# Gate units at three per four key tiles, their high products on VectorE, later transposes, early operand loads and a fourth raw value tile

## The chip, the core and the metric

The program runs on one core of a Trainium2 chip. TensorE (PE in the profile; PEld is its weight loads) multiplies, VectorE (DVE), ScalarE (ACT) and GpSimd (POOL) work on tiles of 128 partitions, and transfers are issued from SyncE's queue (SP) or from GpSimd's. The metric is the device time of one execution in microseconds, the median of several runs.

## The reference, cut

Two layers of attention and feed-forward are followed by two layers of a short convolution or a windowed attention, each with a product-key expert layer ("peer"). Only the two expert layers bear on this change:

```python
q  = (t @ w_q).reshape(n_tok, 8, 2, 128)                   # 256 tokens, 8 heads, 2 halves
sc = einsum("thpd,hpnd->thpn", q, subkeys)                 # 128 keys in each half
sv, si = top_k(sc, 16)
cand = sv[:, :, 0, :, None] + sv[:, :, 1, None, :]         # 16 x 16 pairs of keys
top_v, pos = top_k(cand, 16)
idx = si0[pos] * 128 + si1[pos];  g = softmax(top_v)       # 8 x 16 experts for a token
h = einsum("cd,ced->ce", xc, u_tab[idx])
out = einsum("ce,ced->cd", g * gelu(h), v_tab[idx])
```

## The kernel before

All weights come as 512 KB tiles of 128 partitions by 1024 float32 through one `Stream`. A tile is loaded by SP into a raw tile (L145), ScalarE casts it to a high part `whi` (L156) and VectorE, or GpSimd for tiles marked so in `specs`, subtracts to the low part `wlo` (L165). I call the two together the split. TensorE then takes three products: low weight by high activation, high by low, high by high. In the expert layers there are three raw tiles and three pairs of split tiles (`CAP[0]`), and each is used again in turn; `next` emits the splits up to two tiles ahead of the tile that TensorE is given.

An expert layer (`peer`) is computed densely for 224 of the 256 tokens (`TD`), with gates that are zero where an expert is not chosen; the other 32 tokens (`TG`) fetch their experts' rows by indirect transfers. Its stages follow each other on TensorE:

- **Queries.** Eight pairs of `w_pq` tiles give the queries; `scores` compares them with the keys.
- **Keys.** 128 `peer_u` tiles, the key tiles, give all experts' inner products by `feat_block` (24 matmuls a tile, L505, L506, L510). `keep_h` applies Gelu for each pair of tiles: for tokens without gates yet into `st` (L1549), for the first `td` tokens that have gates into `tmp` (L1552), which VectorE multiplies onto `st` (L1553).
- **Values.** 128 `peer_v` tiles are multiplied by the gated activations (`experts_out`, L1633 and L1636, 16 matmuls a tile).

What is not matrix work of the key stage is written as generators in a list `bg`: `rank_keys` for each head, `rank_pairs` for each block of 128 tokens, then `gates`, then `gather`. After each weight tile `spend` runs them until a budget is used (1.2 after a first tile of a pair, 1.4 after a second); each yield names a cost by which the budget falls. That is the order on every engine, since the program is scheduled by hand.

`rank_pairs` ends with three transposes on TensorE (L1446, L1448) and three copies by VectorE into `ii`, `gg` and `gl` (L1463 to L1465). `gates` works in 56 units of four tokens. For each, VectorE writes two one-hot matrices (L1488), GpSimd multiplies the column one by the gate's high part `gg` (L1490), and the same matrix is multiplied by the low part `gl` on GpSimd for even units (L1492) or by four ScalarE instructions for odd ones (L1497). Two units later TensorE sums them in eight matmuls (L1505, L1506), and the result goes to `st`: by ScalarE where no key tile has been yet (L1513), by VectorE onto what is there (L1515). A unit costs 9.0, so one unit stands after each key tile. The sums lie in PSUM banks named `acc`, the inner products of the keys in banks named `sd`, four of each.

`gather` first loads 32 rows of `x` in four copies and a norm gain into `work` (L290), multiplies them on VectorE (L1583), and then goes through 32 rows of `peer_ur` and 32 of `peer_v`, one 512 KB indirect transfer each (L1574) and one VectorE instruction each (L1589, L1598), over a ring of three tiles. What is left of it is run by `next(rows)` in `experts_out`, one step for each pair of value tiles and a second one where `jj % 16 == 8`.

## Time and profile before

| what | value |
|---|---|
| median of 3 runs | 2541.38 us (2536.73 to 2543.12) |
| the profiled execution | 2538.01 us |
| its span, first to last instruction | 2536.2 us |
| PE, DVE, ACT, POOL busy | 93%, 77%, 51%, 30% of the span |
| moved by DMA | 496.75 MB, 196 GB/s on the mean |

The profiled execution is 1.8 us longer than its span and 3.4 us under the median. The first expert layer lies from 743 to 1575 us of the span and the second from 1697 to 2536 us: two thirds of the whole. The shares of busy time are means over all stages, and VectorE's 77% hides a stage in which it is busy for 95%; so the profile is read by stretches, with TensorE's matmuls counted in each.

### The profile page before, as it was taken

What the parts mean: (1) busy time and instruction counts of PE and PEld (TensorE: products, weight loads), DVE (VectorE), ACT (ScalarE), POOL (GpSimd) and SP (SyncE); (2) the same over time, 40 slices, a digit from 0 to 9 for tenths busy, and PEclk for the clock granted to TensorE, in tenths of its full rate; (3) what the DMA queues carried; (4) which work ended last, traced back from release to release, by engine and by line L of the source; (5) the groups of instructions that cost most, each with busy time, mean ns of one, the idle gap of its engine ahead of it and who ended that gap; (6) DMA issues with size and microseconds to landing.
All of it is one profiled execution on the core that took longest, in us unless ns stands there. A gap on an engine that the chain in (4) does not pass through costs nothing.

```text
span 2536.2 us, 45120 instructions
## 1 busy us (share of the span) xinstructions
PE 2369.3 (93%) x17454; PEld 2224.7 (88%) x17454; DVE 1958.3 (77%) x3386; ACT 1294.3 (51%) x2170; POOL 748.8 (30%) x498
## 2 busy tenths in 40 slices
PE   8999989999999999888999999999999888999998
PEld 6789978899999998888988898889998888988897
DVE  5778776887868989995777776757989995777775
ACT  5555556555544455553444454645445553444454
POOL 0112123111011247663333310411247663333300
PEclk9999999999999999998999999999999998999999
DMA  7345642555545554447888876525654447888874
GB/s 240 100 147 198 209 147 83 173 195 190 180 149 173 183 168 141 143 134 246 297 298 292 289 244 191 170 93 164 189 170 140 143 141 241 301 289 293 302 246 147
DMA packets 141229, 496.75 MB, mean 196 GB/s; under 512 B 17185, under 2 KB 20897, under 8 KB 140754
## 3 DMA queue, kind: packets, MB, share of 16 engines
q1 hardware_dynamic: 121254, 426.11, 51.7%
q0 software_dynamic: 19232, 67.22, 7.3%
q8 instruction: 138, 2.26, 0.4%
q10 hardware_dynamic: 528, 0.52, 0.1%
q14 instruction: 77, 0.63, 0.1%
HBM read 491.07 MB, written 1.08 MB: 194 GB/s over the span
## 4 chain that ended last, share of the span: by engine, by line
PE 46%; DVE 24%; DMA 13%; issue 8%; ACT 7%; POOL 2%; SPq 0%; ACTq 0%; POOLq 0%; DVEq 0%
DMA raw<-peer_v 9%; DVE wlo L165 8%; PE sd L505 7%; PE sd L506 7%; PE sd L510 7%; ACT whi L156 4%; DMA raw<-peer_u 3%; PE acc L300 3%; PE acc L1633 3%; DVE oh L1488 3%; PE acc L301 3%; PE acc L302 3%; PE sd L1633 3%; DVE st L1553 3%; PE acc L1636 2%
## 5 line engine op out<-in xcount | busy, mean ns | idle before, releaser
L156 ACT CAST whi<-raw 128x1024 fp32r<-128x1024 f32 (+1 forms) x776 | 803.4, 1042 | 619.9 <-DMA raw<-peer_v 239.1
L165 DVE TENSOR_TENSOR wlo<-raw,whi 128x1024 fp32r<-128x1024 f32 (+2 forms) x687 | 881.4, 1296 | 301.6 <-ACT whi L156 285.3
L505 PE MATMUL sd<-hTh,wlo 128*128 128x224 f32 (+1 forms) x3176 | 765.8, 283 | 49.2 <-DVE wlo L165 25.5
L506 PE MATMUL sd<-hTl,whi 128*128 128x224 f32 (+1 forms) x3176 | 752.1, 279 | 0.6 <-DVE hTl L306 0.6
L505 PEld LDWEIGHTS sd<-hTh,wlo 128*128 128x128 f32 x3176 | 612.1, 193 | 59.2 <-DVE wlo L165 27.4
L506 PEld LDWEIGHTS sd<-hTl,whi 128*128 128x128 f32 x3176 | 612.1, 193 | 2.9 <-DVE hTl L306 1.0
L510 PE MATMUL sd<-hTh,whi 128*128 128x224 f32 (+1 forms) x3176 | 430.4, 278 | 0.0
L510 PEld LDWEIGHTS sd<-hTh,whi 128*128 128x128 f32 x3176 | 396.5, 192 | 0.0
L165 POOL TENSOR_TENSOR wlo<-raw,whi 128x1024 fp32r<-128x1024 f32 (+1 forms) x89 | 220.5, 2482 | 399.3 <-ACT whi L156 396.0
L1633 PE MATMUL acc<-ahl,whi 128*128 128x448 f32 x1024 | 256.0, 371 | 32.7 <-ACT whi L156 28.0
L1633 PE MATMUL sd<-ahl,whi 128*128 128x448 f32 x1024 | 252.0, 366 | 0.0
L1633 PEld LDWEIGHTS acc<-ahl,whi 128*128 128x128 f32 x1024 | 174.8, 190 | 47.5 <-ACT whi L156 34.0
L1633 PEld LDWEIGHTS sd<-ahl,whi 128*128 128x128 f32 x1024 | 193.0, 188 | 14.5
L1497 ACT ACTIVATE oh<-oh,gl 128x128 f16<-128x128 f16 x224 | 74.1, 431 | 183.7 <-POOL oh L1490 183.7
L1574 POOL DMA_INDIRECT work<-peer_v,idx x64 | 101.0, 1579 | 221.8 <-DVE work L1598 178.1
L1636 PEld LDWEIGHTS acc<-ahl,wlo 128*128 128x128 f32 x1024 | 153.3, 191 | 14.5 <-DVE wlo L165 5.5
L1488 DVE TENSOR_TENSOR oh<-ii,iota 128x512 f16<-128x512 f16 x224 | 161.3, 759 | 0.0
L1636 PE MATMUL acc<-ahl,wlo 128*128 128x224 f32 x1024 | 157.9, 275 | 2.6 <-DVE wlo L165 2.5
L1636 PE MATMUL sd<-ahl,wlo 128*128 128x224 f32 x1024 | 159.0, 276 | 0.0
L1490 POOL TENSOR_TENSOR oh<-oh,gg 128x512 f16<-128x512 f16 x112 | 118.3, 1057 | 117.4 <-DVE oh L1488 98.2
L1574 POOL DMA_INDIRECT work<-peer_ur,idx x64 | 97.6, 1525 | 185.2 <-DVE work L1589 158.0
L1636 PEld LDWEIGHTS sd<-ahl,wlo 128*128 128x128 f32 x1024 | 137.2, 194 | 0.0
(317 smaller groups left out, 3324.5 us busy)
## 6 DMA issues: line engine op xcount, KB each, us to landing
raw<-peer_u SPq DMA_DIRECT2D x256, 512.0 KB
raw<-peer_v SPq DMA_DIRECT2D x256, 512.0 KB
raw<-w_up SPq DMA_DIRECT2D x88, 512.0 KB
raw<-w_down SPq DMA_DIRECT2D x36, 512.0 KB
raw<-w_pq SPq DMA_DIRECT2D x32, 512.0 KB
raw<-w_da SPq DMA_DIRECT2D x24, 512.0 KB
raw<-w_cin SPq DMA_DIRECT2D x24, 512.0 KB
raw<-w_da_o SPq DMA_DIRECT2D x8, 512.0 KB
```

The source lines that it names most:

```text
L156: self.nc.scalar.copy(hi[:, c], raw[:, c])
L165: e.tensor_tensor(lo[:, c], raw[:, c], hi[:, c].bitcast(F32), op=ALU.subtract)
L300: mm(out, sl, mh, start=start, stop=False)
L301: mm(out, sh, ml, start=False, stop=False)
L505: mm(out, lo[:, c], sh[:, kbase + k, ts], start=(k == 0), stop=False)
L506: mm(out, hi[:, c], sl[:, kbase + k, ts], start=False, stop=False)
L510: mm(out, hi[:, c], sh[:, kbase + k, ts], start=False, stop=(k == nk - 1))
L1488: nc.vector.tensor_tensor(o, two(ii[:, c, ts]), bc(self.iota[:, None], [P, 2, P, 2]), op=ALU.is_equal)
L1490: nc.gpsimd.tensor_tensor(high, cols, two(gg[:, ts]), op=ALU.mult)
L1574: nc.gpsimd.indirect_dma_start(out=ring[s % 3], out_offset=None, in_=tables[s // ns], in_offset=off)
L1633: mm(ot[f][:, 0:2 * TD], w[0][:, f * P:(f + 1) * P], a, start=start, stop=stop)
L1636: mm(ot[f][:, 0:TD], w[1][:, f * P:(f + 1) * P], a[:, 0:TD], start=False, stop=False)
```

## The change

Six edits, all in the two expert layers:

- `gates` yields 1.75 in place of 9.0, so that three units stand after four key tiles, and `spend` has 1.5 and 1.7 up to the pair `n` = 19.
- The high products go from GpSimd to VectorE. GpSimd keeps the low products of every fourth unit, and ScalarE takes those of three units in four. GpSimd splits no key tile from the 24th on (before: every fourth of all 128).
- The transposes with their copies become a function `turn`, which is called later: that of the first block between the two halves of the second block's pair ranking, that of the second block after the second gate unit.
- The rows of `x` and the norm gain are loaded at the pair `n` = 11, and not when the gather starts.
- `keep_h` writes Gelu in place, in PSUM, and VectorE multiplies from there; `tmp` goes away.
- `ii`, `gg` and `gl` become parts of one tile `aux`, which, once the gates are done, is a fourth raw tile for every fourth `peer_v` tile. The split tiles stay three.

In `experts_out` a pair's second gather step moves from ahead of the pair to between its two tiles.

```diff
         for j, (_, kind, _) in enumerate(specs):
             k = kind
...
+            x = False
+            if kind == 3:
+                k, fourth = 0, (fourth + 1) % 4
+                x = fourth == 0
+            r, rb = place("x", 1, j) if x else place(("raw", k), self.CAP[k], j)
+            n, nb = place(k, self.CAP[k], j)
+            self.where.append((k, n, x))
+            self.before.append(rb)
+            self.free.append(nb)
...
+        if x and part == 0:
+            return self.extra
...
-            ii = ph.tile([P, 2, TD], F16, name="ii")
-            gg = ph.tile([P, TD], F16, name="gg")
-            gl = ph.tile([P, TD], F32, name="gl")
+            aux = ph.tile([P, D], F32, name="aux")
+            ii = aux[:, 0:TD].bitcast(F16).rearrange("p (c t) -> p c t", c=2)
+            gg = aux[:, TD:TD + TD // 2].bitcast(F16)
+            gl = aux[:, 2 * TD:3 * TD]
...
                     top16([(tv[:, h], posv[:, h], cand[:, h]) for h in range(h0, h0 + 4)])
                     yield 2.4
+                    if turns:
+                        turns.pop()()
...
-                        nc.gpsimd.tensor_tensor(high, cols, two(gg[:, ts]), op=ALU.mult)
-                        if n % 2 == 0:
+                        nc.vector.tensor_tensor(high, cols, two(gg[:, ts]), op=ALU.mult)
+                        if n % 4 == 0:
                             nc.gpsimd.tensor_tensor(cols, cols, two(gl[:, ts]), op=ALU.mult)
-                    if n % 2 == 0 and 0 <= n - 1 < NG:
+                    if n % 4 != 1 and 0 <= n - 1 < NG:
...
-                    yield 9.0
+                    if n == 1:
+                        turns.pop()()
+                    yield 1.75
...
-                    tmp = ph.tile([P, 2, TD], F32, tag="tmp", bufs=1, name=self.nm("tmp"))
-                    nc.scalar.activation(tmp[:, :, 0:td], pv[:, :, 0:td], AF.Gelu)
-                    nc.vector.tensor_tensor(st[:, jj:jj + 2, 0:td], st[:, jj:jj + 2, 0:td], tmp[:, :, 0:td],
+                    nc.scalar.activation(pv[:, :, 0:td], pv[:, :, 0:td], AF.Gelu)
+                    nc.vector.tensor_tensor(st[:, jj:jj + 2, 0:td], st[:, jj:jj + 2, 0:td], pv[:, :, 0:td],
...
-                for q in quarter:
-                    self.load(xr[q], self.x[last, 1])
-                self.load(ring[2], self.ins["ffn_norm_g_2"][layer:layer + 1, :].to_broadcast([P, D]))
                 fetch(0)
                 fetch(1)
-                yield 0.0
...
             for n in range(8 + P // 2):
+                if n == 11:
+                    for q in quarter:
+                        self.load(work[q, 3], self.x[last, 1])
+                    self.load(work[:, 2], self.ins["ffn_norm_g_2"][layer:layer + 1, :].to_broadcast([P, D]))
...
-                        spend(1.2)
+                        spend(1.5 if n < 20 else 1.2)
...
-                        spend(1.4)
+                        spend(1.7 if n < 20 else 1.4)
...
+            self.ws.extra = aux
             self.experts_out(a_split, rows, work[:, 3], area, g_name, g_row, final)
...
-                pool[0] = j % 4 == 1
+                pool[0] = j < 24 and j % 4 == 1
...
-                s.append((i["peer_v"][layer][:, j, :], 0, False))
+                s.append((i["peer_v"][layer][:, j, :], 3, False))
```

The scheduling by hand decides where the units stand. On VectorE, in the middle of the first layer's gates, before (`oh` are the one-hot matrices and products, `wlo` a split tile's low part, `st` the gated activations):

```order
L1488 TENSOR_TENSOR oh_10372<-ii,iota 128x512 x2
L1515 SCALAR_TENSOR_TENSOR st<-acc_11868,st 128x76x4
L165 TENSOR_TENSOR wlo_11930<-raw_11785,whi_11929 128x1024
L1553 TENSOR_TENSOR st<-st,tmp_11960 128x2x120
L1488 TENSOR_TENSOR oh_10372<-ii,iota 128x512
L1488 TENSOR_TENSOR oh_10373<-ii,iota 128x512
L1515 SCALAR_TENSOR_TENSOR st<-acc_11917,st 128x78x4
L1488 TENSOR_TENSOR oh_10373<-ii,iota 128x512 x2
L1515 SCALAR_TENSOR_TENSOR st<-acc_11966,st 128x78x4
L165 TENSOR_TENSOR wlo_12028<-raw_11883,whi_12027 128x1024
```

and now:

```order
L1511 TENSOR_TENSOR oh_10090<-aux,iota 128x512 x2
L1513 TENSOR_TENSOR oh_10090<-oh_10090,aux 128x512
L1538 SCALAR_TENSOR_TENSOR st<-acc_12180,st 128x84x4
L181 TENSOR_TENSOR wlo_12245<-raw_12114,whi_12244 128x1024
L1511 TENSOR_TENSOR oh_10090<-aux,iota 128x512
L1511 TENSOR_TENSOR oh_10091<-aux,iota 128x512
L1513 TENSOR_TENSOR oh_10091<-oh_10091,aux 128x512
L1538 SCALAR_TENSOR_TENSOR st<-acc_12233,st 128x84x4
L181 TENSOR_TENSOR wlo_12290<-raw_12147,whi_12289 128x1024
L1577 TENSOR_TENSOR st<-st,sd_12191 128x2x140
L181 TENSOR_TENSOR wlo_12323<-raw_12196,whi_12322 128x1024
L1511 TENSOR_TENSOR oh_10091<-aux,iota 128x512 x2
```

Each unit has a third product on VectorE, every tile's low part is here, and one tile in four has no unit behind it. On the whole there are 79 low parts on VectorE between the first one-hot matrix and the gather's first product (L1583), where 44 were, and 37 products with Gelu in place of 28. TensorE has the 56 units over 75 key tiles in place of 56 and 15 key tiles behind them in place of 25. The gates begin nine tiles earlier.

On GpSimd, in the first layer's gates, before:

```order
L1490 TENSOR_TENSOR oh_10373<-oh_10373,gg 128x512
L165 TENSOR_TENSOR wlo_11586<-raw_11443,whi_11585 128x1024
L1490 TENSOR_TENSOR oh_10374<-oh_10373,gg 128x512
L1492 TENSOR_TENSOR oh_10373<-oh_10373,gl 128x512
L1490 TENSOR_TENSOR oh_10374<-oh_10374,gg 128x512
```

and now, all that it does from the last index copy to the end of the layer's gather:

```order
L1472 DMA idx<-st 32x32
L1473 DMA gt<-st 32x32
L1515 TENSOR_TENSOR oh_10090<-oh_10090,aux 128x512 x14
L1598 DMA work<-peer_ur,idx 128x1024 x32
L1598 DMA work<-peer_v,idx 128x1024 x32
```

GpSimd's 56 high products, half of its low ones and its splits are gone from the gates. On SP, around the loads of `x` and the gain, before:

```order
L145 DMA raw_13150<-peer_u 128x1024
L145 DMA raw_13183<-peer_u 128x1024
L290 DMA work<-x 32x1024 x4
L290 DMA work<-ffn_norm_g 128x1024
L145 DMA raw_13224<-peer_u 128x1024
```

and now, where they stand 100 rows earlier:

```order
L161 DMA raw_8855<-peer_u 128x1024
L161 DMA raw_8886<-peer_u 128x1024
L306 DMA work<-x 32x1024 x4
L306 DMA work<-ffn_norm_g 128x1024
L161 DMA raw_8932<-peer_u 128x1024
```

They have moved past some 100 key tiles, from the gather's start into the ranking of the keys.

## Rows read from the trace of the kernel before

**Rows 1.** By stretches, L505 alone: length, PE, PEld busy (count), clock, DMA share, GB/s
```profile
795.80:938.00 142.20, 91.48 (x384) 75.90 (x385) 0.96 0.58 179
938.00:1141.00 203.00, 105.78 (x441) 84.48 (x442) 1.00 0.47 141
1141.00:1170.20 29.20, 12.96 (x48) 10.50 (x48) 0.77 0.74 229
1170.20:1225.40 55.20, 35.13 (x152) 29.13 (x152) 1.00 0.79 269
1749.80:1888.00 138.20, 88.88 (x384) 73.81 (x384) 1.00 0.59 180
1888.00:2093.00 205.00, 105.58 (x441) 84.28 (x441) 1.00 0.46 142
2093.00:2122.50 29.50, 13.17 (x48) 10.67 (x48) 0.77 0.72 225
```

**Rows 2.** Unbroken stretches, all engines: length, PE, PEld, DVE, ACT, POOL, clock, DMA, GB/s
```profile
786.00:806.00 20.00, 20.00 (x178) 20.00 (x177) 15.85 (x75) 10.77 (x17) 2.39 (x1) 1.00 0.52 159
1500.00:1550.00 50.00, 50.00 (x321) 47.74 (x320) 31.78 (x32) 27.05 (x31) 0.00 (x0) 1.00 0.69 218
```

**Rows 3.** Timeline of PE: a gate unit's first matmul, and the next key tile's
```profile
1109.13 0.23 PE L1505 MATMUL acc<-oh 128*128 128x128 f16 x1
...
1109.62 0.35 PE L505 MATMUL sd<-hTh,wlo 128*128 128x224 f32 x1
```

**Rows 4.** Ranking and gates of the first layer, all engines, columns as in rows 2
```profile
763.00:938.00 175.00, 169.33 (x1457) 168.34 (x1456) 149.94 (x511) 86.02 (x113) 38.14 (x24) 0.97 0.56 175
938.00:1141.00 203.00, 182.69 (x1766) 177.53 (x1764) 193.72 (x227) 111.81 (x270) 141.36 (x95) 1.00 0.47 141
```

**Rows 5.** Waits from 770 to 938 us: us in total, times, longest
```profile
PE sd L1448 <- DVE st L1442: 4.8, 2, 3.0
```

**Rows 6.** Groups, 928 to 1147 us: busy us, mean ns | idle, releasers
```profile
L1488 DVE TENSOR_TENSOR oh<-ii,iota 128x512 f16<-128x512 f16 x112 | 79.8, 752 | 0.0
L165 DVE TENSOR_TENSOR wlo<-raw,whi 128x1024 fp32r<-128x1024 f32 x45 | 78.6, 1746 | 13.6 <-ACT whi L156 7.8 <-issue 5.4 <-ACT st L1549 0.4
L1553 DVE TENSOR_TENSOR st<-st,tmp 128x16 f32<-128x16 f32 (+27 forms) x28 | 32.8, 1172 | 0.0
...
L1490 POOL TENSOR_TENSOR oh<-oh,gg 128x512 f16<-128x512 f16 x56 | 58.7, 1048 | 59.6 <-DVE oh L1488 48.9 <-PE acc L1506 8.5 <-DVE st L1515 2.2
L1492 POOL TENSOR_TENSOR oh<-oh,gl 128x512 f16<-128x512 f16 x28 | 52.4, 1870 | 2.2
...
L1497 ACT ACTIVATE oh<-oh,gl 128x128 f16<-128x128 f16 x112 | 37.0, 430 | 89.6 <-POOL oh L1490 89.6
```

**Rows 7.** By line: shortest/median/longest ns; last row a group, 1147 to 1225 us
```profile
L1488 DVE TENSOR_TENSOR oh<-ii,iota x224: 407/412/2610, 928.8 to 2089.9; 128x512 f16<-128x512 f16 x112
L1515 DVE SCALAR_TENSOR_TENSOR st<-acc,st x112: 345/457/576, 942.4 to 2096.1; 128x192 f32<-128x192 f32 x4, 128x200 f32<-128x200 f32 x4, 128x208 f32<-128x208 f32 x4, 128x216 f32<-128x216 f32 x4
L1553 DVE TENSOR_TENSOR st<-st,tmp x80: 601/1115/2785, 947.5 to 2175.8; 128x448 f32<-128x448 f32 x26, 128x16 f32<-128x16 f32 x2, 128x32 f32<-128x32 f32 x2, 128x48 f32<-128x48 f32 x2
...
L165 DVE TENSOR_TENSOR wlo<-raw,whi 128x1024 fp32r<-128x1024 f32 x18 | 21.8, 1222 | 21.7 <-ACT whi L156 21.7
```

**Rows 8.** Waits at the gather's start, 1138 to 1176 us
```profile
DVE work L1583 <- DMA work<-ffn_norm_g: 12.0, 1, 12.0
```

**Rows 9.** Value stage, all engines: both layers with gather, and the fullest 25 us
```profile
1225.40:1475.00 249.60, 234.32 (x1444) 219.47 (x1445) 188.05 (x207) 113.74 (x134) 79.02 (x50) 0.99 0.84 294
2180.40:2430.00 249.60, 235.41 (x1455) 218.70 (x1455) 189.56 (x207) 113.58 (x135) 78.40 (x50) 1.00 0.84 296
2378.50:2403.50 25.00, 24.35 (x151) 22.55 (x150) 20.14 (x20) 10.73 (x13) 8.84 (x6) 1.00 0.92 329
```

**Rows 10.** Ranking, L165 alone: DVE and POOL busy (count)
```profile
763.00:938.00 175.00, 55.23 (x45) 30.99 (x13) 0.97 0.56 175
```

**Rows 11.** Issues of the loads of `x` on SP: shortest, median, longest ns
```profile
L290 SPq DMA_DIRECT2D work<-x x8: 527/603/1199, 1147.2 to 2101.6; - x8
```

More of the change, by code (lines that the diff above doesn't have):

```diff
@@ L117, in __init__, with place @@
         self.todo = []
-        self.where, self.before = [], []
-        seq = [[], [], []]
-        ring = 0
+        self.where, self.before, self.free = [], [], []
+        seq = {}
+        ring = fourth = 0
+        def place(key, cap, j):
+            q = seq.setdefault(key, [])
+            q.append(j)
+            return (len(q) - 1) % cap, q[-1 - cap] if len(q) > cap else -1
         for j, (_, kind, _) in enumerate(specs):
@@ L125, in __init__ @@
                 k = 1 if kind and ring >= self.CAP[0] else 0
-            self.where.append((k, len(seq[k]) % self.CAP[k]))
-            self.before.append(seq[k][-self.CAP[k]] if len(seq[k]) >= self.CAP[k] else -1)
-            seq[k].append(j)
+            x = False
[7 more added lines that the diff above has]
+            self.free.append(nb)
     def widen(self, pool):
@@ L168, in _open @@
     def _open(self, j):
-        k = self.where[j][0]
-        return (self.local if k == 2 else self.pools[k]) is not None
+        k, _, x = self.where[j]
+        return (self.extra if x else self.local if k == 2 else self.pools[k]) is not None
     def fill(self, n=None):
@@ L178, in _ready @@
         j = self.n_split
-        return j < self.n_dma and j < self.i + lead and self.before[j] < done
+        return j < self.n_dma and j < self.i + lead and self.free[j] < done
     def ahead(self, n, held):
@@ L1443, in rank_pairs @@
                 yield 0.6
-                pt = self.bank()
-                for c in range(2):
-                    nc.tensor.transpose(pt[:, c * P:(c + 1) * P], sel[:, c].rearrange("p h k -> p (h k)"),
-                                        self.ident)
-                nc.tensor.transpose(pt[:, 2 * P:3 * P], ge.rearrange("p h k -> p (h k)"), self.ident)
                 if tb == 1:
@@ L1459, in rank_pairs, with turn @@
                         nc.gpsimd.dma_start(gt[q], gef[last, q])
-                n = min(P, TD - tb * P)
-                ts = slice(tb * P, tb * P + n)
-                pi, pg = pt[:, 0:2 * P].rearrange("p (c t) -> p c t", c=2)[:, :, 0:n], pt[:, 2 * P:2 * P + n]
-                nc.vector.tensor_copy(ii[:, :, ts], pi)
-                nc.vector.tensor_copy(gg[:, ts], pg)
-                nc.vector.tensor_tensor(gl[:, ts], pg, gg[:, ts], op=ALU.subtract)
-                yield 0.8
+                def turn():
+                    pt = self.bank()
+                    for c in range(2):
+                        nc.tensor.transpose(pt[:, c * P:(c + 1) * P], sel[:, c].rearrange("p h k -> p (h k)"),
+                                            self.ident)
+                    nc.tensor.transpose(pt[:, 2 * P:3 * P], ge.rearrange("p h k -> p (h k)"), self.ident)
+                    n = min(P, TD - tb * P)
+                    ts = slice(tb * P, tb * P + n)
+                    pi, pg = pt[:, 0:2 * P].rearrange("p (c t) -> p c t", c=2)[:, :, 0:n], pt[:, 2 * P:2 * P + n]
+                    nc.vector.tensor_copy(ii[:, :, ts], pi)
+                    nc.vector.tensor_copy(gg[:, ts], pg)
+                    nc.vector.tensor_tensor(gl[:, ts], pg, gg[:, ts], op=ALU.subtract)
+                turns.append(turn)
+            turns = []
             state = {"j": 0, "t": 0, "b": 0.0}
@@ L1642, in experts_out @@
             nxt = a_split(jj + 2)
-            next(rows, None)
-            if jj % 16 == 8:
-                next(rows, None)
             for c in range(2):
+                if c == 0 or jj % 16 == 8:
+                    next(rows, None)
                 w = self.ws.next()
@@ L1681, in experts_out @@
         self.ws.ahead(2, 0)
+        self.ws.extra = None
         turn(1)
```

4 lines of the change are left out of this document (2 added, 2 removed).

## The prediction

> **What bounds the kernel now.** I looked first at the two expert layers by stretches, counting the L505 matmuls in each, because these are eight to a key tile and so turn a stretch into a number of tiles [rows 1]. Then I took a price for a tile from a stretch in which TensorE never stops [rows 2]: 178 matmuls in 20 us, 24 to a tile, so 2.70 us for a key tile; 321 in 50 us, 16 to a tile, so 2.49 us for a value tile. A gate unit adds 9.62 - 9.13 = 0.49 us on TensorE [rows 3]. The reader is to see how far each stretch lies above its price:
>
> - Ranking: 384/8 = 48 tiles, 48 x 2.70 = 129.6 us; measured 142.2 and 138.2. Lost: 12.6 and 8.6.
> - Gates: 55 tiles, each with a unit, 55 x 3.19 = 175.5; measured 203 and 205. Lost: 27.5 and 29.5.
> - Start of the gather: 6 tiles and the last unit, 16.7; measured 29.2 and 29.5. Lost: 12.5 and 12.8. The granted clock is 0.77 there.
> - The next 19 tiles: 51.3; measured 55.2. Lost: 3.9, which nothing in the change aims at.
> - Values with gather [rows 9]: 1444/16 = 90.3 tiles, 224.7 us, and 1455/16 = 90.9, 226.4; measured 249.6 each. Lost: 24.9 and 23.2.
>
> So some 81 us in each layer are time in which TensorE, the bound, waits, or runs at a lower clock after a wait. What it waits for differs by stretch. In the gates VectorE is busy for 193.7 of 203 us [rows 4], and its instructions are long: a low part takes 1746 ns on the mean where it takes 1222 after the gates, a one-hot matrix 752 where the shortest take 407, a product with Gelu 1172 where the shortest, of the full width, takes 601 [rows 6, 7]. GpSimd is busy for 141 us of the same stretch, and ScalarE stands for 89.6 us behind GpSimd's high products [rows 4, 6]. In the ranking TensorE waits twice for the last step before the transposes [rows 5]. At the gather's start VectorE waits 12.0 us for the gain, with the low parts of the next tiles queued behind it [rows 8].
>
> **The change part by part.**
>
> *Gates.* They take 75 tiles now: 75 x 2.70 + 56 x 0.49 = 229.9 us on TensorE. VectorE, at undisturbed durations [rows 7]: 75 low parts x 1.22 = 91.5; 56 units x three products x 0.41 = 68.9; 56 x 0.457 (L1515) = 25.6; 37 products with Gelu x 0.4 = 15 (they grow from almost nothing to 0.60; 22 if all were of the full width). Sum 201. The third product has no row on VectorE; it has L1488's size and types and the same kind of broadcast, so I take 0.41, with 0.75, L1488's mean in company, as the other end (+19). The product that reads PSUM has no row of its own either; L1515 reads PSUM too and is not slow, so I take the price of L1553 undisturbed. GpSimd keeps 14 products of 1.87 [rows 6]; each may hold VectorE for nothing or for its whole length, 0 to 26; I take 20, near the upper end, because VectorE's instructions are long exactly where GpSimd works. That makes 221 of TensorE's 230 us: tight, but under it. ScalarE gets 14 units more at 37.0/28 = 1.32 us, 18.5, and 20 more casts, 21, to 151 of 230, and its wait for GpSimd goes. Gelu into PSUM I price like Gelu into `tmp`; its bank stays taken until VectorE's product, which is covered by the other three banks, and an uncovered wait would be that product's 0.6 us a pair. Lost after: 5 us, between 0 and 23.
>
> *Ranking.* Nine tiles fewer stand beside the same ranking. VectorE's part without the low parts is 149.9 - 55.2 = 94.7 us [rows 4, 10], of which some 4 are the first gate units and 4 to 11 time lost to GpSimd's splits, half of which remain; I take 87. 40 low parts x 1.23 = 49. Together 136 us beside 49 tiles, whose TensorE time is 175 - 12.6 - 9 x 2.70 = 138. VectorE goes from 86% to nearly full, so I do not expect the loss to vanish: 8 us a layer, between 3 and 15. Deferring the transposes removes the 4.8 us of waits [rows 5] and the slow clock behind them; they still cost TensorE the same three matmuls, and VectorE's three copies wait for these with the next low part queued behind them, which one unit of lead covers.
>
> *Loads of `x` and the gain.* VectorE's wait of 12.0 us goes. What is late next is the first gathered row, which GpSimd can issue before VectorE reaches it. Lost at the start after: 1.5 us, between 0 and 5. The five transfers, 1 MB, now stand in SP's queue in front of key tiles in the ranking: about five issues of 0.6 us [rows 11] and, at the 329 GB/s of rows 9, 3.2 us of transfer. A raw tile is asked for three tiles ahead, so most of it is hidden; 1 us, between 0 and 4.
>
> *Fourth raw tile.* Its load must wait for the gates' last reader, some 15 tiles earlier, so that costs nothing. A pair of value tiles and 9/8 of a gathered row are 1.64 MB, in 4.98 us 329 GB/s. The stretches moved 294 and 296, the fullest 25 us 329 [rows 9]; there 151 matmuls took 25 us, 1.5 above price. Five more gather steps fall into this stage (58 for 53), so 270 us at that loss make 16; with no loss 0. A transfer may now be asked for one tile, 2.49 us, earlier, which hides single late ones; I take 9, nearer the middle. The row with 329 GB/s shows what was moved, not a ceiling. The Trainium skill (HBM Reference, Specifications) gives a core about 358 GB/s when its neighbour streams too and about 425 alone; by that the demand fits, the loss would be 0 and the time 18 us shorter. No 25 us of this trace show more than 329, so no run here shows that figure.
>
> **The sum.** First layer: 4.6 (ranking) - 1 (loads) + 22.5 (gates) + 11.0 (start) + 15.9 (values) = 53.0. Second: 0.6 - 1 + 24.5 + 11.3 + 14.2 = 49.6. The profiled execution took 2538.0 us, 3.4 under the median of the runs and within their spread of 6.4: 2538.0 - 102.6 = 2435.4, so 2436.
>
> **The rivals.**
>
> *VectorE becomes the bound in gates and ranking.* If the third product takes 0.75 and GpSimd blocks fully, the gates need 246 to 253 us on VectorE, 23 lost, and the ranking loses 15: 25 us more a layer, 2486. For it: VectorE at 96% in my own sum. Against it: L1488's 407 ns for the same shape. The Trainium skill (VectorE: DVE Perf Modes, What auto-detection actually checks) says that a two-input instruction runs at double rate when all tensors are 16-bit with unit step, as `gg` and the one-hot matrices are; by that 0.41 holds and this rival falls back on GpSimd alone.
>
> *The values stay bound by transfers.* The fourth tile only moves the wait: 15.9 + 14.2 come back, and five more rows a layer at the same loss (24.9/53 each) add 5: 2471. For it: DMA is 84% busy over the whole stretch. Against it: 92% with little loss in the fullest 25 us.
>
> *Slower than before.* GpSimd's remaining products, now beside more VectorE work, keep every VectorE instruction at its long duration: 75 x 1.746 + 56 x (3 x 0.752 + 0.457) + 37 x 1.172 = 326 us in the gates, 96 over TensorE's price where 27.5 to 29.5 were lost, while the other parts still give 30.5 and 25.1: 38 and 42 us worse a layer, 2618. It decides from about 3.84 us a tile, (230 + 58)/75, on. Against it: GpSimd's work there falls from 141 us to 26.
>
> *Everything hides.* The taken losses (8, 1, 5, 1.5, 9) shrink to 3, 0, 0, 0, 0: 21.5 a layer more, 2393.
>
> That the change does not do what it says: the order of instructions shows the units, products, loads and the fourth tile where the diff puts them, so this has no chance of its own.
>
> **How the numbers follow.** Forecast 2436: 0.52 (by itself 2415 to 2458); values bound by transfers 2471: 0.20; VectorE bound 2486: 0.12; everything hides 2393: 0.10; slower 2618: 0.04; losses of several kinds that leave it within 0.3% of before: 0.02. The range of 2400 to 2495 holds the first three and half of the fourth. 0.3%, 7.6 us, is about what a measurement of this kernel can tell from no change. Faster 0.94, same 0.02, slower 0.04.
>
> **What would show it.** In the profile after: a pattern of tiles of 3.2 and 2.7 us in the gates, low parts at about 1.22 us and one-hot matrices near 0.41 on VectorE, and no wait of ScalarE for GpSimd beyond 14 products. No wait of VectorE for the gain, and a clock at 1.0 at the gather's start. In the ranking, VectorE nearly full and no wait of TensorE for L1442's step; if TensorE waits for low parts there by more than 15 us, the ranking's term is wrong. In the values, more than 310 GB/s while rows are gathered and less than 10 us of waits of TensorE for `whi`. The prediction is wrong if the gates take above 240 us for their 75 tiles, or the values stay at 2.75 us a tile.

## The result and the profile after

The changed kernel takes 2422.97 us (median of 4 runs, 2421.45 to 2424.66), the kernel before 2539.06 beside it: ratio 0.9546, 95% interval 0.9522 to 0.957. The forecast of 2436 is 13 us too long, the range of 2400 to 2495 holds the time. The profiled execution took 2421.45 us. Its page gives the busy engines and the chain that ended last:

```profile
PE 2335.8 (97%) x17454; PEld 2210.4 (91%) x17454; DVE 1899.1 (78%) x3558; ACT 1347.1 (56%) x2302; POOL 440.4 (18%) x306
...
PE 82%; DVE 9%; issue 3%; ACT 3%; DMA 2%; POOL 1%; SPq 0%; POOLq 0%; DVEq 0%; ACTq 0%
```

GpSimd fell from 30% to 18% of the span, and the chain is TensorE's own work for 82%. The counterpart of [rows 1] counts the first of the key tiles' matmuls (now L521; lines from L145 on have moved by 16, in the gates by 23), eight to a tile. Each layer's stretches are the ranking, the gates, the gather's start and the tiles up to the values (length; PE, PEld busy and count; clock, DMA share, GB/s):

```profile
794.90:912.00 117.10, 71.64 (x304) 58.88 (x305) 0.99 0.58 177
912.00:1143.60 231.60, 142.07 (x600) 114.96 (x600) 1.00 0.58 178
1143.60:1159.70 16.10, 11.10 (x48) 9.21 (x48) 1.00 0.68 220
1159.70:1186.00 26.30, 16.53 (x72) 13.82 (x72) 1.00 0.89 302
1686.70:1806.20 119.50, 72.85 (x304) 59.75 (x305) 0.97 0.56 176
1806.20:2037.40 231.20, 142.08 (x601) 114.98 (x601) 1.00 0.58 178
2037.40:2053.40 16.00, 11.08 (x48) 9.17 (x48) 1.00 0.67 222
2053.40:2081.70 28.30, 16.53 (x72) 13.82 (x72) 1.00 0.88 305
```

The counterparts of [rows 4] and [rows 9], all engines (PE, PEld, DVE, ACT, POOL): the first layer's ranking, its gates, both value stages and 25 us of one.

```profile
767.00:912.00 145.00, 135.13 (x1168) 133.70 (x1168) 133.86 (x490) 68.36 (x89) 17.94 (x8) 0.99 0.57 175
912.00:1143.60 231.60, 230.24 (x2250) 228.88 (x2249) 191.14 (x336) 163.35 (x373) 20.59 (x23) 1.00 0.58 178
...
1186.00:1475.00 289.00, 288.98 (x1839) 275.21 (x1840) 234.88 (x258) 149.94 (x174) 94.77 (x56) 1.00 0.89 313
2081.70:2371.00 289.30, 289.26 (x1834) 276.14 (x1835) 234.63 (x258) 149.18 (x172) 95.69 (x56) 0.99 0.88 309
1400.00:1425.00 25.00, 25.00 (x161) 23.82 (x160) 21.15 (x21) 12.75 (x15) 11.73 (x6) 1.00 0.91 332
```

At the prediction's prices (2.70 us a key tile, 0.49 a unit, 2.49 a value tile) the losses are, first layer / second:

| stretch | lost before | forecast | measured |
|---|---|---|---|
| ranking, with the moved loads | 12.6 / 8.6 | 9 | 117.1 - 38 x 2.70 = 14.5 / 16.9 |
| gates, 75 tiles and 56 units | 27.5 / 29.5 | 5 | 231.6 - 229.9 = 1.7 / 1.3 |
| gather start, 6 tiles | 12.5 / 12.8 | 1.5 | 16.1 - 16.2, none / none |
| tiles up to the values (9; 19 before) | 3.9 / 54.5 - 51.3 = 3.2 | as before | 26.3 - 24.3 = 2.0 / 4.0 |
| values, 115 tiles | 24.9 / 23.2 | 9 | 289.0 - 286.2 = 2.8 / 3.9 |

The measured losses sum to 47.1 where 56.1 were forecast. Behind the ranking everything came out better than taken, but for the second layer's last key tiles (4.0 for 3.2). The ranking came out worse than taken, even worse than before.

The groups of the gates, 912 to 1143 us, answer [rows 6, 7]:

```profile
L181 DVE TENSOR_TENSOR wlo<-raw,whi 128x1024 fp32r<-128x1024 f32 x76 | 100.4, 1321 | 38.5 <-ACT whi L172 38.3
L1520 ACT ACTIVATE oh<-oh,aux 128x128 f16<-128x128 f16 x168 | 55.3, 431 | 1.9 <-DVE oh L1513 1.7
L1511 DVE TENSOR_TENSOR oh<-aux,iota 128x512 f16<-128x512 f16 x110 | 41.4, 418 | 0.0
...
L1513 DVE TENSOR_TENSOR oh<-oh,aux 128x512 f16<-128x512 f16 x56 | 23.8, 425 | 1.9
L1515 POOL TENSOR_TENSOR oh<-oh,aux 128x512 f16<-128x512 f16 x14 | 14.6, 1041 | 197.4 <-DVE oh L1513 183.1 <-PE acc L1529 14.3
```

VectorE's instructions are back near their undisturbed lengths, and ScalarE's 89.6 us behind GpSimd [rows 6] are gone: its products now wait 1.9 us, for VectorE (L1520).

### The profile page after: what moved, and what is told of

Its sections match the earlier page's. It is cut to its first block, busy times and chain, and to the rows that moved or that the text cites. A ratio compares the mean times of both kernels' runs of the same rounds, so it can differ in the third digit from the quotient of the medians.

```text
span 2419.7 us, 45185 instructions
## 1 busy us (share of the span) xinstructions
PE 2335.8 (97%) x17454; PEld 2210.4 (91%) x17454; DVE 1899.1 (78%) x3558; ACT 1347.1 (56%) x2302; POOL 440.4 (18%) x306
## 4 chain that ended last, share of the span: by engine, by line
PE 82%; DVE 9%; issue 3%; ACT 3%; DMA 2%; POOL 1%; SPq 0%; POOLq 0%; DVEq 0%; ACTq 0%
PE sd L521 13%; PE sd L526 12%; PE sd L522 12%; PE acc L1658 9%; PE sd L1658 9%; PE sd L1661 5%; PE acc L1661 5%; PE acc L316 3%; PE acc L317 3%; PE acc L318 3%; DVE wlo L181 3%; DMA raw<-peer_u 1%; PE acc L1528 1%; ACT whi L172 1%; PE acc L1529 1%
## 5 line engine op out<-in xcount | busy, mean ns | idle before, releaser
L181 DVE TENSOR_TENSOR wlo<-raw,whi 128x1024 fp32r<-128x1024 f32 (+2 forms) x675 | 833.6, 1250 | 183.9 <-ACT whi L172 182.6
L172 ACT CAST whi<-raw 128x1024 fp32r<-128x1024 f32 (+3 forms) x712 | 736.6, 1042 | 422.1 <-PE sd L526 245.8
L521 PE MATMUL sd<-hTh,wlo 128*128 128x224 f32 (+1 forms) x3176 | 761.9, 282 | 23.8 <-DVE wlo L181 20.8
L521 PEld LDWEIGHTS sd<-hTh,wlo 128*128 128x128 f32 x3176 | 609.2, 192 | 30.3 <-DVE wlo L181 19.0
L1658 PE MATMUL acc<-ahl,whi 128*128 128x448 f32 x1024 | 251.1, 366 | 5.8 <-DVE ahl L322 5.8
L321 ACT CAST ahl<-st 128x448 fp32r<-128x448 f32 x128 | 72.4, 567 | 234.6 <-PE sd L1661 234.5
L1658 PEld LDWEIGHTS acc<-ahl,whi 128*128 128x128 f32 x1024 | 174.3, 190 | 13.9 <-DVE ahl L322 6.2
L322 DVE TENSOR_TENSOR ahl<-st,ahl 128x448 fp32r<-128x448 f32 x128 | 79.7, 624 | 101.4 <-ACT ahl L321 101.1
L1598 POOL DMA_INDIRECT work<-peer_v,idx x64 | 112.9, 1764 | 168.3 <-DVE work L1618 144.3
L181 POOL TENSOR_TENSOR wlo<-raw,whi 128x1024 fp32r<-128x1024 f32 (+1 forms) x37 | 93.5, 2537 | 268.5 <-ACT whi L172 265.3
L1520 ACT ACTIVATE oh<-oh,aux 128x128 f16<-128x128 f16 x336 | 110.5, 430 | 3.2 <-DVE oh L1513 2.9
```

Source lines behind the costliest of these rows:

```text
L172: self.nc.scalar.copy(hi[:, c], raw[:, c])
L181: e.tensor_tensor(lo[:, c], raw[:, c], hi[:, c].bitcast(F32), op=ALU.subtract)
L322: self.nc.vector.tensor_tensor(lo, src, hi.bitcast(F32), op=ALU.subtract)
L521: mm(out, lo[:, c], sh[:, kbase + k, ts], start=(k == 0), stop=False)
L1520: nc.scalar.activation(cols[i], cols[i], AF.Copy, scale=gl[:, 4 * n - 4 + t:4 * n - 3 + t])
L1598: nc.gpsimd.indirect_dma_start(out=ring[s % 3], out_offset=None, in_=tables[s // ns], in_offset=off)
```

## The experiments

Each is an edit of the changed kernel, shown against it. To compare runs I read the start of every tile from its first weight load and take its length less the price (2.69 for a key tile, 3.67 where scores stand behind a pair of query tiles, 0.50 for a unit, 2.505 for a value tile). "To first unit" runs from the layer's first query tile, so it is a little more than the table above has.

Each of these runs but the last was timed once. The times of one kernel differ by up to 17 us over all runs (the kernel before: 2531.76 to 2548.39), so that a single time close to another decides nothing, and the losses have to. They spread too. Seven runs leave the work up to the first unit as it is, but for the first products of e1, e5 and e9 (the changed kernel, e1, e2, e3, e5, e7, e9); they lose 16.2 to 18.2 us there in the first layer and 14.5 to 19.2 in the second, with medians of 17.7 and 17.5. The changed kernel's own 16.2 and 19.2 are two ends of these ranges, so what an edit is worth there is taken from the medians. In the row of e12 the time is the median of four runs, and the losses are those of the one that took 2395.5.

| run | time, us | to first unit | gates | from there to the values | values |
|---|---|---|---|---|---|
| before | 2538.0 | 13.9 / 10.7 | 27.6 / 29.7 | 17.6 / 16.9 | 25.3 / 23.2 |
| changed | 2421.5 | 16.2 / 19.2 | 2.3 / 1.8 | 2.2 / 4.2 | 1.2 / 1.9 |
| e1 high products on GpSimd | 2424.9 | 17.8 / 18.8 | 3.2 / 5.1 | 2.2 / 2.2 | 1.2 / 1.2 |
| e2 a unit at each tile | 2427.0 | 17.7 / 17.2 | 2.2 / 2.1 | 2.1 / 2.1 | 1.2 / 2.7 |
| e3 three raw tiles | 2464.0 | 17.6 / 17.7 | 2.0 / 1.8 | 2.2 / 4.2 | 24.4 / 20.6 |
| e4 loads at the gather | 2430.4 | 13.6 / 12.2 | 2.8 / 1.8 | 13.0 / 12.4 | 2.7 / 1.6 |
| e5 old units | 2466.2 | 17.8 / 16.2 | 18.4 / 18.4 | 4.8 / 5.6 | 2.8 / 3.4 |
| e6 splits all along | 2438.9 | 18.1 / 18.2 | 1.8 / 2.1 | 8.7 / 8.5 | 3.9 / 2.7 |
| e7 Gelu through SBUF | 2419.2 | 17.1 / 14.5 | 2.2 / 1.8 | 2.2 / 2.2 | 1.2 / 1.2 |
| e8 no GpSimd splits | 2418.4 | 13.9 / 15.0 | 2.1 / 2.0 | 5.6 / 2.5 | 2.6 / 1.2 |
| e9 loaded and spaced | 2429.2 | 18.2 / 17.5 | 5.5 / 4.7 | 2.2 / 3.4 | 1.2 / 2.7 |
| e10 old budgets | 2402.5 | 9.7 / 9.6 | 0.9 / 0.9 | 2.2 / 2.2 | 1.8 / 2.7 |
| e12 three edits | 2400.4 | 7.2 / 6.9 | 0.8 / 0.8 | 2.2 / 2.2 | 1.2 / 1.2 |

### What made the gates long

**e1**, the high products back on GpSimd:

```diff
-                        nc.vector.tensor_tensor(high, cols, two(gg[:, ts]), op=ALU.mult)
+                        nc.gpsimd.tensor_tensor(high, cols, two(gg[:, ts]), op=ALU.mult)
```

> The changed kernel with one edit: the high products go back to GpSimd, the units stay at three per four tiles. Theory A, the gates were long because GpSimd's work blocks VectorE: GpSimd has 56 products of about 1.04 us and 14 low ones again, some 73 us in the 230 us of the gates, low parts on VectorE go from 1.22 us to above 1.4, and the gates lose 15 to 30 us a layer against the 2 lost now; 2455 to 2480 us. Theory B, the spacing alone gave the room: the gates lose under 8 us a layer, 2425 to 2438 us.

**e2**, the old spacing:

```diff
-                    yield 1.75
+                    yield 9.0
```

> The changed kernel with one edit: a unit costs 9.0 again, so one stands after each key tile, with the high products still on VectorE. Theory A, GpSimd's blocking was the cause: VectorE needs 1.22 + 3 x 0.42 + 0.47 + 0.22 = 3.17 us a tile beside TensorE's 3.19, and 14 GpSimd products add up to 15 us, so the gates' 56 tiles lose 3 to 15 us a layer; 2425 to 2450 us. Theory B, the spacing was what mattered: they lose 25 us or more a layer as before the change; 2470 us or more.

Neither brings the loss back: 3.2 and 5.1 us in e1, where theory A had 15 to 30, and 2.2 and 2.1 in e2, where theory B had 25 or more. The theory that one of the two alone had made the gates long fell twice.

**e5**, all three edits to the units undone (that of e1, that of e2, and the low products of every second unit on GpSimd):

```diff
...
-                        if n % 4 == 0:
+                        if n % 2 == 0:
                             nc.gpsimd.tensor_tensor(cols, cols, two(gl[:, ts]), op=ALU.mult)
-                    if n % 4 != 1 and 0 <= n - 1 < NG:
+                    if n % 2 == 0 and 0 <= n - 1 < NG:
...
```

> The changed kernel with all three of the units' edits undone: high products on GpSimd, low products on GpSimd for every second unit (28 a layer), one unit after each key tile. What stays of the change in the gates is that GpSimd splits no key tile there and that Gelu writes into PSUM. GpSimd then has about 56 x 1.05 + 28 x 1.9 = 112 us of work in the 180 us of the gates, where the kernel before had 141 of 203. Theory A (the splits on GpSimd of every fourth key tile were what made the gates long; the units' own products are borne): the gates lose under 8 us a layer, time 2418 to 2435. Theory B (the sum of GpSimd's work beside VectorE counts, whichever it is; high and low products are most of it): the gates lose 15 to 28 us a layer, time 2448 to 2478.

**e9**, as e5 but with the new spacing kept:

> The changed kernel with all products of the units on GpSimd again (56 high, 28 low a layer) but with its three units in four key tiles kept. Against the run with the old units this changes the spacing alone: GpSimd has the same 110 us or so of work, in 231 us in place of 197. Theory A (what counts is GpSimd's share of the time, so that the spacing is worth something once GpSimd is loaded): the gates lose 3 to 9 us a layer, time 2425 to 2440. Theory B (each product on GpSimd costs the same wherever it stands): they lose 14 to 19 us a layer, time 2450 to 2465.

**e6**, GpSimd's splits kept to the end:

```diff
-                pool[0] = j < 24 and j % 4 == 1
+                pool[0] = j % 4 == 1
```

> The changed kernel with GpSimd splitting every fourth key tile to the end again, as before; everything else of the change stays. GpSimd gets 19 splits in the gates, 2.5 to 3.4 us each, and VectorE has 19 low parts less. Theory A (these splits alone made the gates long): the gates lose 18 to 28 us a layer, time 2455 to 2478. Theory B (it takes the splits together with the products of the units on GpSimd): VectorE has slack with 19 low parts less, the gates lose 2 to 10 us a layer, time 2420 to 2440.

e5 loses 18.4 us a layer in the gates: theory B, it takes the load. e9 differs from it by the spacing alone and loses 5.5 and 4.7: theory A. e6 loses no more in the gates than the changed kernel: theory B, a little under its size. In the gates of the first layer, from each run's groups and windows:

| run | GpSimd busy | VectorE busy | low part, ns | one-hot, ns | product with Gelu, ns | units per tile | lost, us |
|---|---|---|---|---|---|---|---|
| before | 144.2 of 205 | 95% | 1785 | 761 | 1215 | 1 | 27.6 |
| e5 | 114.9 of 196 | 92% | 1735 | 619 | 365 | 1 | 18.4 |
| e9 | 116.8 of 235 | 85% | 1524 | 550 | 375 | 3/4 | 5.5 |
| e1 | 89.2 of 232 | 81% | 1474 | 495 | 375 | 3/4 | 3.2 |
| e6 | 63.2 of 231 | 75% | 1329 | 462 | 378 | 3/4 | 1.8 |
| e2 | 20.8 of 180 | 91% | 1351 | 416 | 371 | 1 | 2.2 |
| changed | 20.6 of 232 | 83% | 1321 | 418 | 379 | 3/4 | 2.3 |

VectorE's instructions grow with GpSimd's share of the time, as the prediction said, but for small steps among the last three rows. But VectorE's busy share isn't what decides: e2 has 91% and loses 2.2, e5 has 92% and loses 18.4. The timeline of e5 shows the difference (start, us, engine, line; in brackets idle time before and what ended it):

```profile
997.86 1.90 POOL L1515 TENSOR_TENSOR oh<-oh,aux 128x512 f16<-128x512 f16 x1
...
999.81 0.22 PE L1528 MATMUL acc<-oh 128*128 128x128 f16 x1 [0.43 <-POOL oh L1515]
...
1000.55 1.04 POOL L1513 TENSOR_TENSOR oh<-oh,aux 128x512 f16<-128x512 f16 x1 [0.79 <-PE acc L1529]
1000.62 2.05 DVE L181 TENSOR_TENSOR wlo<-raw,whi 128x1024 fp32r<-128x1024 f32 x1
...
1003.74 1.04 POOL L1513 TENSOR_TENSOR oh<-oh,aux 128x512 f16<-128x512 f16 x1 [2.15 <-PE acc L1529]
...
1004.15 1.71 DVE L181 TENSOR_TENSOR wlo<-raw,whi 128x1024 fp32r<-128x1024 f32 x1 [0.23 <-ACT whi L172]
...
1004.86 1.90 POOL L1515 TENSOR_TENSOR oh<-oh,aux 128x512 f16<-128x512 f16 x1
...
1006.81 0.22 PE L1528 MATMUL acc<-oh 128*128 128x128 f16 x1 [0.45 <-POOL oh L1515]
```

TensorE and GpSimd wait for each other in turn. TensorE's sums wait for a low product of 1.90 us that ended just before (1004.86 + 1.90 = 1006.76), and GpSimd's next high product waits for these sums. With a unit at each tile there is no slack in this ring: the tiles go 3.2, 3.8, 3.2, 3.8 us, the long one where the low product is GpSimd's. The waits over the gates of e5 and then of e9, us in total, times, longest:

```profile
ACT oh L1520 <- POOL oh L1513: 76.4, 28, 5.0
...
POOL oh L1513 <- PE acc L1529: 27.8, 25, 2.2
...
PE acc L1528 <- POOL oh L1515: 12.4, 20, 2.4
```

```profile
POOL oh L1513 <- PE acc L1529: 56.4, 17, 4.5
...
ACT oh L1520 <- POOL oh L1513: 16.9, 13, 5.4
...
PE acc L1528 <- POOL oh L1515: 3.0, 1, 3.0
```

With one tile in four free of a unit, the same GpSimd work makes TensorE wait once in place of 20 times. GpSimd still waits for the sums, even longer (56.4 us), but that is idle time of an engine ahead of its work and costs TensorE nothing. So what had made the gates long was GpSimd's load and a spacing without slack together: of e5's 18.4 us, taking away the load takes 16 (e2), giving slack 13 (e9). e9 also lowers GpSimd's share of the time, from 59% to 50%; that the ring and not this share decides is read from the waits and was not tried by itself. Which buffer makes the high product wait for the sums was not tried either.

The kernel before loses some 10 us a layer more than e5, and has the splits and Gelu in SBUF besides; no run parts these two at that load. Its own trace speaks for the splits. These are all of TensorE's waits of its first gates, 935 to 1140 us:

```profile
PE acc L1505 <- POOL oh L1492: 10.7, 23, 0.9
PE sd L505 <- POOL wlo L165: 9.6, 12, 0.9
```

The first line is the ring of e5. The second is GpSimd's low part of every fourth tile, which comes late for TensorE. TensorE never waited for VectorE there: VectorE's long instructions, on which the prediction rests, reach it only by way of GpSimd, whose high products wait 48.9 us for the one-hot matrices [rows 6].

e6 loses behind the gates, where its splits stand beside the gather's start: 8.7 and 8.5 us there where the changed kernel has 2.2 and 4.2. That is what leaving out the later splits is worth there.

**e7**, Gelu through a tile in SBUF:

```diff
-            gl = aux[:, 2 * TD:3 * TD]
+            gl = aux[:, 3 * TD // 2:5 * TD // 2]
...
-                    nc.scalar.activation(pv[:, :, 0:td], pv[:, :, 0:td], AF.Gelu)
-                    nc.vector.tensor_tensor(st[:, jj:jj + 2, 0:td], st[:, jj:jj + 2, 0:td], pv[:, :, 0:td],
+                    tmp = aux[:, 5 * TD // 2:9 * TD // 2].rearrange("p (c t) -> p c t", c=2)
+                    nc.scalar.activation(tmp[:, :, 0:td], pv[:, :, 0:td], AF.Gelu)
+                    nc.vector.tensor_tensor(st[:, jj:jj + 2, 0:td], st[:, jj:jj + 2, 0:td], tmp[:, :, 0:td],
                                             op=ALU.mult)
```

> The changed kernel with Gelu written to a tile in SBUF again and multiplied from there, in place of PSUM. Theory A (the place of Gelu's result matters, since in the kernel before that product took 1.17 us and now 0.3 to 0.6): the product takes 0.9 to 1.2 us and with 37 of them VectorE gains 20 to 30 us of work in the gates; VectorE, at 191 of 231 us now, gets to 215, and the gates lose 5 to 15 us a layer, time 2428 to 2450. Theory B (that product was long only because GpSimd worked beside it): it stays under 0.65 us and the time within 5 us of 2423.

The time is the same, and so is the product, shortest, median and longest ns over the program:

```profile
L1578 DVE TENSOR_TENSOR st<-st,aux x88: 162/435/623, 931.1 to 2079.0; 128x448 f32<-128x448 f32 x14, 128x16 f32<-128x16 f32 x2, 128x24 f32<-128x24 f32 x2, 128x40 f32<-128x40 f32 x2
```

Theory B: where GpSimd is almost idle, PSUM or SBUF is one price (the changed kernel has a median of 430 ns). Beside a busy GpSimd it isn't: 1215 ns from SBUF in the kernel before, 365 from PSUM in e5.

### The fourth raw tile

**e3**:

```diff
-                s.append((i["peer_v"][layer][:, j, :], 3, False))
+                s.append((i["peer_v"][layer][:, j, :], 0, False))
```

> The changed kernel without its fourth raw tile: all value tiles go through the three raw tiles, the gather is untouched. Theory A, the fourth tile is what removed the waits of the value stage: 20 to 25 us a layer come back and the stage moves about 295 GB/s while rows are gathered; 2463 to 2475 us. Theory B, the later and evener gather steps removed them: under 8 us a layer come back; 2425 to 2440 us.

The loss of before is back, 24.4 and 20.6 us (theory A; the time of 2464.0 is in its range). Both value stages of e3 (columns as in the counterpart of rows 9), then the waits of the first:

```profile
1188.00:1477.00 289.00, 274.01 (x1689) 256.39 (x1690) 219.87 (x243) 133.71 (x158) 91.03 (x56) 0.99 0.84 293
2105.60:2394.90 289.30, 277.37 (x1716) 260.58 (x1717) 222.33 (x245) 134.15 (x159) 88.22 (x56) 0.99 0.84 296
```

```profile
ACT whi L172 <- DMA raw<-peer_v: 119.3, 65, 4.5
...
PE acc L1658 <- ACT whi L172: 15.0, 16, 1.9
```

In the changed kernel the same stretch has:

```profile
ACT whi L172 <- DMA raw<-peer_v: 11.9, 23, 1.2
ACT whi L172 <- DMA aux<-peer_v: 8.9, 13, 2.2
```

TensorE's 15.0 us of waits for casts are gone, and ScalarE's waits for the transfers fall from 119.3 us to 20.8. Three raw tiles move 293 and 296 GB/s, four 313 and 309: what bounded the stage was how early a transfer can be asked for.

### What the ranking loses

**e4**, the loads of `x` and the gain back at the gather:

```diff
+                for q in quarter:
+                    self.load(xr[q], self.x[last, 1])
+                self.load(ring[2], self.ins["ffn_norm_g_2"][layer:layer + 1, :].to_broadcast([P, D]))
                 fetch(0)
                 fetch(1)
+                yield 0.0
...
-                if n == 11:
-                    for q in quarter:
-                        self.load(work[q, 3], self.x[last, 1])
-                    self.load(work[:, 2], self.ins["ffn_norm_g_2"][layer:layer + 1, :].to_broadcast([P, D]))
```

> The changed kernel with the loads of x and the gain back at the gather's start. The start loses about 12 us a layer again by every theory. Theory A, the 13 us that the ranking loses now come from these loads standing in front of key tiles: the ranking loses under 6 us a layer, the sum is 2423 + 24 - 14, 2430 to 2436 us. Theory B, VectorE is full in the ranking, whatever the loads: the ranking loses 11 to 15 us as now; 2443 to 2449 us.

Neither theory fits: the ranking still loses 13.6 and 12.2 us, as theory B had it, but the time, 2430.4, is theory A's. Against the medians of the seven runs the early loads cost the ranking 4.1 and 5.3 us, a part of its loss and not most of it, and they save 10.8 and 8.2 behind the gates. In e4 the gather's start in the first layer, and VectorE's wait in it (L1607 is the product with the gain):

```profile
1141.10:1165.40 24.30, 18.74 (x148) 18.55 (x146) 11.58 (x13) 7.70 (x11) 3.36 (x2) 0.86 0.64 185
```

```profile
DVE work L1607 <- DMA work<-ffn_norm_g: 8.8, 1, 8.8
```

**e8**, no key tile split on GpSimd:

```diff
-                pool[0] = j < 24 and j % 4 == 1
+                pool[0] = False
```

> The changed kernel with no key tile split on GpSimd at all: the six that it still splits beside the ranking go to VectorE, 6 x 1.25 = 7.5 us more there. Theory A (the ranking loses its 16 to 19 us a layer because VectorE is simply full): it loses up to 7 us more, time 2423 to 2437. Theory B (GpSimd's splits are what hurts: a split takes 2.5 to 3.4 us where VectorE takes 1.25, and VectorE's ranking steps beside it are longer): the ranking loses 4 to 10 us a layer less, time 2403 to 2415.

Against the medians the ranking loses 3.8 and 2.5 us less, the second within the spread of the seven runs: theory B's direction, under its size of 4 to 10, and the time, 2418.4, lies in neither range. One VectorE step beside such a split, in the changed kernel:

```profile
839.44 3.36 POOL L181 TENSOR_TENSOR wlo<-raw,whi 128x1024 fp32r<-128x1024 f32 x1 [9.46 <-ACT whi L172]
840.60 4.34 DVE L1439 TENSOR_TENSOR st<-st 128x2048 f16<-128x2048 f16 x1
...
844.87 1.21 DVE L181 TENSOR_TENSOR wlo<-raw,whi 128x1024 fp32r<-128x1024 f32 x1
...
846.13 0.37 PE L521 MATMUL sd<-hTh,wlo 128*128 128x224 f32 x1 [4.28 <-DVE wlo L181]
```

In e8 the same step has, shortest, median, longest:

```profile
L1439 DVE TENSOR_TENSOR st<-st x4: 2291/2292/2293, 842.5 to 1775.2; 128x2048 f16<-128x2048 f16 x4
```

VectorE's 4.34 us are 2.20 until the split ends (842.80) and 2.14 behind it. TensorE waits 4.28 us for the low part queued behind.

**e10**, the ranking given out as thinly as before:

```diff
-                        spend(1.5 if n < 20 else 1.2)
+                        spend(1.2)
...
-                            spend(1.7 if n < 20 else 1.4)
+                            spend(1.4)
```

> The changed kernel with the ranking's work given out as thinly as before: the budget per half of a pair of key tiles back at 1.2 and 1.4 from the first tile, in place of 1.5 and 1.7. The ranking ends some tiles later, the units begin later, and there are 14 tiles behind them that take this up. Theory A (the ranking loses its 16 to 19 us a layer because VectorE is given too much at a time): everything up to the first unit loses 5 to 12 us a layer, time 2405 to 2418. Theory B (the loss comes at single long steps of VectorE, longer than the lead of two tiles, which a budget doesn't divide): it loses 14 to 19 as now, time within 4 us of 2423.

Theory A: 9.7 and 9.6 us, which is 8.0 and 7.9 under the medians; the time, 2402.5, is even under its range. The units begin 8 tiles later, and what is given up behind them (8 of the 9 tiles between the gather's start and the values) had saved nothing. A part of the gain is where the steps fall: L1439 takes 2291 to 2293 ns all four times in e10, so it meets no split there, though GpSimd still has its six. Counted as in the first table, over 46 tiles up to the gates:

```profile
794.90:927.00 132.10, 85.48 (x368) 70.66 (x368) 1.00 0.58 188
1678.90:1810.80 131.90, 86.24 (x368) 71.39 (x368) 0.99 0.60 192
```

46 x 2.70 = 124.2, so 7.9 and 7.7 lost.

**e11**, the transposes in place:

> The changed kernel with the transposes back at the end of the ranking of the pairs, where TensorE waits in turn for the ranking's last step. Theory A (the deferral takes away the waits of 4.8 us a pass, and the slow clock behind them): everything up to the first unit loses 3 to 8 us a layer more than now, time 2428 to 2440. Theory B (the wait was time in which VectorE caught up with its low parts, and comes back as a wait for these): within 4 us of 2423.

It took 4618.7 us, and says nothing of the transposes. In this one run TensorE went at a lower rate from start to end and was busy for 99% of it, while VectorE's low part and ScalarE's cast kept their medians (1225 and 1047 ns, in the changed kernel 1221 and 1049). The same matmul in it and in the changed kernel, shortest, median, longest ns:

```profile
L522 PE MATMUL sd<-hTl,whi x3176: 369/387/545, 262.8 to 3965.4; 128*128 128x224 f32 x128, 128*128 128x256 f32 x71
```

```profile
L522 PE MATMUL sd<-hTl,whi x3176: 268/275/420, 147.7 to 2076.7; 128*128 128x224 f32 x128, 128*128 128x256 f32 x71
```

Its weight loads have a median of 376 ns in place of 192. Its trace holds no rows of the granted clock, so the reason stays open, and so does what deferring the transposes is worth.

**e12**, three edits together:

```diff
-                if n == 11:
+                if n == 44:
...
-                        spend(1.5 if n < 20 else 1.2)
+                        spend(1.2)
...
-                            spend(1.7 if n < 20 else 1.4)
+                            spend(1.4)
...
-                pool[0] = j < 24 and j % 4 == 1
+                pool[0] = False
```

> The changed kernel with three edits together that the runs point to: the old budgets, no key tile split on GpSimd, and the loads of the gathered tokens' operands in the middle of the gates (at the pair of key tiles numbered 44 in place of 11). With the old budgets alone the stretch up to the first unit loses 9.7 and 9.6 us, and the run was 2402.5 us. Theory A (the three act on different losses of that stretch: waits for transfers that the early loads push back, and VectorE's and TensorE's waits beside GpSimd's splits): it loses 4 to 7 us a layer, time 2391 to 2399. Theory B (what is left after the thinner budget is VectorE's long steps alone, and six low parts more on it take back what the loads give): 8 to 11 us a layer, time 2399 to 2406.

2400.43 us (2395.48 to 2402.49), ratio to before 0.9449, interval 0.9433 to 0.9465: faster than both kernels. The stretch loses 7.2 and 6.9 us, at theory A's upper end, and 2.5 to 2.7 less than e10; the median time lies where B had it. The gain over e10 rests on these losses, since e10 has a single time, and it is no larger than the spread of the seven runs in the second layer. The three edits overlap: alone they give 8.0, 4.1 and 3.8 us in the first layer and 7.9, 5.3 and 2.5 in the second, together 10.5 and 10.6. TensorE's waits up to the first unit of the first layer, changed kernel and e12:

```profile
PE sd L521 <- DVE wlo L181: 9.7, 6, 4.3
```

```profile
PE sd L521 <- DVE wlo L181: 3.1, 3, 1.9
```

## Why the prediction held, point by point

**The sum** was right within 13 us because errors of both signs met in it: behind the ranking 12.9 us too much loss in the first layer and 9.5 in the second (gates, start, tiles, values), in the ranking 5.5 and 7.9 too little. That the size came so near is in part luck. The difference is 9.0 of the 14 us by which the profiled execution is shorter than the sum's 2435.4; the rest lies outside these stretches and in the rounding of the prices.

**Gates**: right in the main. The third product took 0.425 us where 0.41 was taken. The term that was mis-sized is the 20 us for GpSimd's remaining products: they take 1041 ns each, not 1.87 us, 14.6 in all, and the low parts grew by 100.4 - 76 x 1.22 = 7.7. Added up as the prediction adds them, VectorE's instructions come to 100.4 + 110 x 0.418 + 56 x 0.425 + 55 x 0.465 (L1538) + 13.7 (L1577) = 209 us, where 221 were taken. (Its busy time is less, 191, since the records of neighbouring instructions overlap.) The reason given for the old loss, VectorE's length beside GpSimd, was one of two conditions: e5 and e9 show the other, the spacing, and TensorE's waits before were for GpSimd itself.

**Ranking**: the step that failed. VectorE's sum of 136 us was right (136.7 busy from 762.1 to 912 us, a stretch that begins as far ahead of the first key tile as that of [rows 4]), but it was taken, beside TensorE's 138, as all there is to the loss: with the same work beside 38 key tiles in place of 48, the loss was to fall to 8 us. e10, which takes back the higher budgets alone, prices them at 8.0 and 7.9 us; the loads, at 1 us between 0 and 4, took 4.1 and 5.3 (e4). Without the budgets the loss is 7.9 and 7.7 in the prediction's count, loads included, where 8 and 1 were taken. What the sum leaves out are single waits of TensorE for a low part that stands behind a long step of VectorE: 9.7 us in six waits now, and before

```profile
PE sd L505 <- DVE wlo L165: 0.9, 2, 0.5
```

Behind the longest of them, the one that ends at 846.13, TensorE went at the lower level of its clock (columns as in the counterpart of rows 9):

```profile
847.00:850.40 3.40, 3.40 (x19) 3.40 (x17) 3.30 (x6) 0.00 (x0) 0.00 (x0) 0.51 0.96 312
```

The prediction's own sign of a wrong term, more than 15 us of such waits, was not met (9.7 and 9.8), though the term came out too small by 5.5 and 7.9. VectorE's busy share doesn't tell these cases apart: it is 92% in the changed kernel's ranking (133.9 of 145 us), and 92% in that of e12, which loses less than half as much:

```profile
780.00:924.30 144.30, 141.04 (x1248) 140.03 (x1246) 132.25 (x450) 72.62 (x91) 2.18 (x5) 1.00 0.55 182
```

**Gather start**: right; no wait for the gain, clock 1.00, and no loss. **Transposes**: the wait of [rows 5] is no longer among TensorE's waits; its worth wasn't measured.

**Values**: mechanism right, size wrong: 2.8 and 3.9 in place of 9. The 9 came from taking the loss at 329 GB/s as partly the transfers' own. The tiles fit at 313 and 309 GB/s on the mean, 332 in the 25 us shown, without TensorE waiting. Here the rule cited from the Trainium skill (HBM Reference, Specifications) pointed the right way: by it the loss was 0. Its figures themselves are shown by no run.

**Rivals**: behind the ranking "everything hides" came nearest; "values bound by transfers" is what e3 shows without the fourth tile. A VectorE that becomes the bound did not come in the gates, where TensorE waits once in the first layer, for 1.4 us and for GpSimd. In the ranking the 15 us that this rival named did come (14.5 and 16.9 with the loads), though not by VectorE's share, as e12 shows. A VectorE kept long by GpSimd did not come: GpSimd was busy for 20.6 us of the gates.

## What to carry to other kernels

Before an engine's load is blamed, look whether two engines wait for each other in turn around it: an idle slot in the pattern can be worth nearly as much as a lighter load (13 us in e9, 16 in e2, of e5's 18.4). Where work is given out by a budget, price the budget itself: beginning a later stage sooner is worth nothing if there is slack behind it (e10). Look for single long steps ahead of a short one that the bound engine needs; a sum of busy time does not show them. A stage whose cast waits for its transfers well under the highest rate seen may want one more buffer, not less traffic (e3).
